# Two mixer layers: level products from 64-row halves, an early copy of one projection, softmax statistics in pairs

## The chip, the cores and the metric

One Trainium2 chip, one NeuronCore. The number is device time in microseconds of one execution of the whole program. TensorE (PE) does the matrix products, VectorE (DVE) and ScalarE (ACT) the element-wise work and everything that leaves PSUM, GpSimd (POOL) some element-wise work between SBUF tiles, SyncE (SP) issues the loads.

## The reference

A float32 model block for 256 tokens and a width of 1024: two layers of a first kind (indexed attention beside a gated delta rule), then two layers of a second kind. The second kind is what is changed. Each of its two layers does

```python
u = rms_norm(h) @ w_in                      # split into the inputs of four mixers
o_a = nsa_attention(...)                    # 4 heads of 64: compressed + selected + window
o_b = diff_attention(...)                   # 4 heads, two softmax maps each, p0 - lam * p1
o_c = gla_mixer(...)                        # 4 heads, key width 32   } chunked gated
o_d = hgrn2_mixer(...)                      # 4 heads, key width 64   } linear attention
h = h + concat(o_a, o_b, o_c, o_d) @ w_out
```

and then a feed-forward part: dense in the first of the two layers, eight experts (two per token) in the second. The two gated linear attentions are, per head, `o_t = sum over s <= t of (q_t . k_s * exp(b_t - b_s)) v_s` within chunks of 64 and a carried state between chunks, with `b` the running sum of the log gates. The differential attention normalises its queries and keys (16 groups of 32 per token) before its products.

## The kernel before, in words

All weight products (`proj_tok`, `proj_ch`, `mm3` at lines 150 to 154) are done as three passes over a high and a low half of the operands; ACT casts the high half (L142) and DVE, or POOL for every fourth one in the mixer layers (`gp_every`), subtracts the low half (L145). The program is written in order with priorities; a planner then fixes the order of the instructions on each engine, and each engine runs its own list strictly in that order. So an instruction that waits holds back all that stands behind it on its engine.

`block2_mixers` (L1186) is run twice. In it:

- **Differential projection** (`ev_dqk`, L1216): for each of the two token tiles the 512 columns in PSUM are squared by ACT, summed by DVE, raised to -1/2 by POOL (`powm`), and then multiplied by DVE straight from PSUM (L1224). The PSUM tile is one of three (`pmm`) that all projections share.
- **Maps** (`softmax_map`, L1410; `nsa_a`, `diff_a`): eight items per layer, four of each kind, each with two logit tiles. Each logit tile gets its own maximum (DVE, L1413), scaling (DVE, L1414) and two exponentials with a running sum (ACT, L1418); then come reciprocals and scalings per tile, transposes (PE, L1426) and the product with the values (PE, L1459, L1495). An item's first half is put ahead of the second half of the item before it (`staggered`). The maps have a priority ahead of the levels.
- **Levels** (L1616): the causal matrix within blocks of 128 tokens is built in seven levels with half-widths s = 1, 2, 4, ..., 64, and one product for the two blocks against each other (`Ex`, L1663 on). At each level, decays `E` are formed by two subtractions (DVE, L1624 and L1626) and one exponential over both halves (ACT, L1631); the decayed keys `Kt` are written by POOL (L1634); the decayed queries `Q` by DVE (L1636); `queries` (L1605) spreads them by six ACT copies (L1610 four, L1613 two) into zero-filled tiles `qbg`, `qbh`, in which each head has a column block of its own with only its rows filled. The products (L1647 for `gla`, L1649 for `hgrn2`) then contract over all 128 rows. Their results go from the two `gd` buffers of PSUM into `AT`: by four predicated copies of DVE (L1659) for s up to 16, by ACT copies (L1655) for 32 and 64. So one level's results must leave before the next level's products may start. `AT` itself is first filled with the diagonal: `pgk`, a product on POOL (L1588), small matrix products into `dg`, and two POOL instructions of 128x1024 (L1599).
- The output `gpo` (L1716) takes `AT`, and the result goes through `w_out` (`tile_T`, `proj_tok`).
- Weight loads of later stages wait for their buffers, which come free as the projections are split.

Of the kernel before, what the change touches and what calls it, by code (L numbers as in the profile page):

```python
# [10 lines left out]
F32 = mybir.dt.float32  # L11
# [1114 lines left out]
def level_tiles(k):  # L1126

    k.qbg = k.lvl.tile([P, 2, 4, P], F32, tag="qbg", name="qbg")
    k.qbh = k.lvl.tile([P, 2, 2, 2, P], F32, tag="qbh", name="qbh")
    k.AT = k.lvl.tile([P, 2, 8, P], F32, tag="AT", name="AT")  # L1130
    k.nc.gpsimd.memset(k.qbg, 0.0)
    k.nc.gpsimd.memset(k.qbh, 0.0)


def prepare_b2(k):
# [25 lines left out]
    for l, r in enumerate(k.r2):  # L1161
        lam_init = 0.8 - 0.6 * math.exp(-0.3 * l)
        nc.vector.tensor_scalar(r.on[:, 0, :], r.on[:, 0, :], 1.0 - lam_init, None, op0=ALU.mult)
        lv = r.lam.rearrange("p (a b d) -> p a b d", a=2, b=2)
        pr = cp.tile([P, 2, 32], F32, name=f"lamp{l}")
        nc.vector.tensor_tensor(pr, lv[:, :, 0, :], lv[:, :, 1, :], op=ALU.mult)
        s2 = cp.tile([P, 2], F32, name=f"lams{l}")
        nc.vector.tensor_reduce(s2, pr, axis=AX.X, op=ALU.add)
        nc.scalar.activation(s2, s2, AF.Exp)
        r.nlam = cp.tile([P, 1], F32, name=f"nlam{l}")  # L1170
        nc.vector.tensor_sub(r.nlam, s2[:, 1:2], s2[:, 0:1])
        nc.vector.tensor_scalar(r.nlam, r.nlam, lam_init, None, op0=ALU.subtract)

# [12 lines left out]
def block2_mixers(k, a, l, hl, pre):  # L1186
# [5 lines left out]
    with ExitStack() as es:  # L1192
# [23 lines left out]
        def ev_dqk(tt, ps):  # L1216
            sq = n2("dsq").rearrange("p (g d) -> p g d", d=32)
            nc.scalar.activation(sq, ps.rearrange("p (g d) -> p g d", d=32), AF.Square)
# [4 lines left out]
            dqk = n2("dqk").rearrange("p (g d) -> p g d", d=32)  # L1223
            nc.vector.tensor_tensor(dqk, ps.rearrange("p (g d) -> p g d", d=32),  # L1224
                                    r[:, :, None].to_broadcast([P, 16, 32]), op=ALU.mult)
# [184 lines left out]
        def softmax_map(lp, S, n, sc, name):  # L1410

            mx = sm.tile([P, n], F32, tag="mx", name="mx", bufs=8)
            nc.vector.tensor_reduce(mx, lp, axis=AX.X, op=ALU.max)  # L1413
            nc.vector.tensor_scalar(mx, mx, -sc, None, op0=ALU.mult)  # L1414
            su = sm.tile([P, n], F32, tag="su", name="su", bufs=12)
            pr = n2(name).rearrange("p (n s) -> p n s", n=n)
            for j in range(n):
                nc.scalar.activation(pr[:, j, :S], lp[:, j, :], AF.Exp, scale=sc, bias=mx[:, j : j + 1],  # L1418
                                     accum_out=su[:, j : j + 1])
            return pr, su  # L1420
# [11 lines left out]
        def nsa_a(kind, tt, m):  # L1432
# [9 lines left out]
            r = []  # L1442
            for j in range(2):
                pr, su = softmax_map(lps[j][:, :, :S], S, 2, 0.125, "npr")
                nc.vector.reciprocal(su, su)
                nc.vector.tensor_tensor(su, su, g3[:, tt, 2 * m + j, 1:3], op=ALU.mult)
                r.append((pr, su))
            return r
# [18 lines left out]
        def diff_a(kind, tt, par):  # L1467
# [10 lines left out]
            e0, s0 = softmax_map(lps[0][:, :, :S], S, 2, dsc, "de0")  # L1478
            e1, s1 = softmax_map(lps[1][:, :, :S], S, 2, dsc, "de1")
            nc.vector.reciprocal(s1, s1)  # L1480
            nc.vector.scalar_tensor_tensor(s1, s1, r2.nlam, s0, op0=ALU.mult, op1=ALU.mult)
            nc.vector.reciprocal(s0, s0)
# [5 lines left out]
        def diff_b(r, kind, tt, par):  # L1488
# [12 lines left out]
            if par == 1:  # L1501
# [8 lines left out]
                for g in range(4):  # L1510
                    o = mv[:, g]
                    nc.vector.scalar_tensor_tensor(o, o, ss[:, g : g + 1], r2.on[:, 0, :], op0=ALU.mult, op1=ALU.mult)
# [9 lines left out]
        gcat = one.tile([P, 3, T], F32, name="gcat")  # L1522
        gf = lambda t: t.rearrange("p a t -> p (a t)")
# [64 lines left out]
        nc.gpsimd.tensor_tensor(pgk, qcat, kcat, op=ALU.mult)  # L1588
        dgp = gdt("dg")[:, :16].rearrange("p (t h) -> p t h", t=2)
        for tt in range(2):  # L1590
            sl = slice(tt * P, (tt + 1) * P)
            nc.tensor.matmul(dgp[:, tt, 0:4], pgk[:, 0, sl], c["bd32"], start=True, stop=True)
            for cb in range(2):
                nc.tensor.matmul(dgp[:, tt, 4 + 2 * cb : 6 + 2 * cb], pgk[:, 1 + cb, sl], c["bd64"],
                                 start=True, stop=True)
        dg = one.tile([P, 2, 8], F32, name="dg")
# [6 lines left out]
        AX_ = one.tile([P, 8, P], F32, name="ATx")  # L1603

        def queries(i, src):  # L1605

            Qg, Qh = k.qbg[:, i % 2], k.qbh[:, i % 2]
            for h in range(4):
                rows = slice(32 * h, 32 * h + 32)
                nc.scalar.copy(Qg[rows, h, :], src[rows, 0, :])  # L1610
# [3 lines left out]
            return Qg, Qh  # L1614

        for i, s in enumerate(LEVELS):  # L1616
# [3 lines left out]
            bv, Ev = pv(b_), pv(E)  # L1620
            if s == 64:
                nc.scalar.activation(Ev[:, :, 1, :], bv[:, :, 1, :], AF.Exp)
            else:
                nc.vector.tensor_tensor(Ev[:, :, 1, :], bv[:, :, 1, :],  # L1624
                                        bv[:, :, 0, s - 1 : s].to_broadcast([P, npair, s]), op=ALU.subtract)
            nc.vector.tensor_tensor(Ev[:, :, 0, :], bv[:, :, 0, s - 1 : s].to_broadcast([P, npair, s]),  # L1626
                                    bv[:, :, 0, :], op=ALU.subtract)
            if s == 64:
                nc.scalar.activation(Ev[:, :, 0, :], Ev[:, :, 0, :], AF.Exp)
            else:  # L1630
                nc.scalar.activation(E, E, AF.Exp)  # L1631

            Kt = Kts[i % 2]
            nc.gpsimd.tensor_tensor(pv(Kt)[:, :, 0, :], pv(kcat)[:, :, 0, :], Ev[:, :, 0, :], op=ALU.mult)  # L1634
            Q = sm.tile([P, 3, P], F32, tag="Q", name="Q")
            nc.vector.tensor_tensor(gf(Q).rearrange("p (n s) -> p n s", s=s), pv(qcat)[:, :, 1, :], Ev[:, :, 1, :],  # L1636
                                    op=ALU.mult)
            Qg, Qh = queries(i, Q)
            od4 = lambda ap: ap.rearrange("p h (b two s) -> p h b two s", two=2, s=s)[:, :, :, 1, :]
            bs = lambda ap: ap.rearrange("p (b s) -> p b s", s=s)  # L1640
            bs4 = lambda ap: ap.rearrange("p h (b s) -> p h b s", s=s)
            pg = gdt("pg").rearrange("p (t h i) -> p t h i", t=2, h=4)
            ph = gdt("ph").rearrange("p (t h i) -> p t h i", t=2, h=4)
            for tt in range(2):
                sl = slice(tt * P, (tt + 1) * P)
                hs = slice(tt * 64, (tt + 1) * 64)
                nc.tensor.matmul(pg[:, tt], Kt[:, 0, sl], Qg[:, :, hs], start=True, stop=True)  # L1647
                for cb in range(2):
                    nc.tensor.matmul(ph[:, tt, 2 * cb : 2 * cb + 2], Kt[:, 1 + cb, sl], Qh[:, cb, :, hs],  # L1649
                                     start=True, stop=True)  # L1650
            for o, ps in ((0, pg), (4, ph)):
                if s >= 32:

                    for b in range(0, P, 2 * s):
                        nc.scalar.copy(k.AT[b : b + s, :, o : o + 4, b + s : b + 2 * s],  # L1655
                                       ps[b : b + s, :, :, b // 2 : b // 2 + s])
                    continue
                for tt in range(2):
                    nc.vector.copy_predicated(od4(k.AT[:, tt, o : o + 4, :]),  # L1659
                                              bs(k.lvm[s])[:, None].to_broadcast([P, 4, 64 // s, s]),  # L1660
                                              bs4(ps[:, tt]))
# [12 lines left out]
        nc.gpsimd.tensor_tensor(Kt[:, :, :P], kcat[:, :, :P], E[:, :, :P], op=ALU.mult)  # L1674
        Q = sm.tile([P, 3, P], F32, tag="Q", name="Qx")
        nc.vector.tensor_tensor(Q, qcat[:, :, P:], E[:, :, P:], op=ALU.mult)
        Qg, Qh = queries(len(LEVELS), Q)
        pg = gdt("pgx").rearrange("p (h i) -> p h i", h=4)
        ph = gdt("phx").rearrange("p (h i) -> p h i", h=4)
        nc.tensor.matmul(pg, Kt[:, 0, :P], Qg, start=True, stop=True)  # L1680
        for cb in range(2):
            nc.tensor.matmul(ph[:, 2 * cb : 2 * cb + 2], Kt[:, 1 + cb, :P], Qh[:, cb], start=True, stop=True)
# [475 lines left out]
```

## Time and profile before

| | us |
|---|---|
| three runs, median (lowest to highest) | 2425.89 (2424.93 to 2430.03) |
| profiled execution, whole | 2425.61 |
| its span, first to last instruction | 2423.5 |
| first mixer layer, in the span | about 693 to 890 |
| second mixer layer, in the span | about 1163 to 1345 |
| mean granted TensorE clock | 0.986 of full speed |

A busy share is the time in which an engine had an instruction under way. A busy PE is not a PE at its peak, and it counts time at the lower clock in full. Idle time of an engine is named after what ended it. Times in the rows below are microseconds from the start of the span unless a column says ns. Line numbers are those of the kernel before.

### The profile page before, as it was taken

What the parts mean: (1) busy time and instruction counts of PE and PEld (TensorE: products, weight loads), DVE (VectorE), ACT (ScalarE), POOL (GpSimd) and SP (SyncE); (2) the same over time, 40 slices, a digit from 0 to 9 for tenths busy, and PEclk for the clock granted to TensorE, in tenths of its full rate; (3) what the DMA queues carried; (4) which work ended last, traced back from release to release, by engine and by line L of the source; (5) the groups of instructions that cost most, each with busy time, mean ns of one, the idle gap of its engine ahead of it and who ended that gap; (6) DMA issues with size and microseconds to landing.
All of it is one profiled execution on the core that took longest, in us unless ns stands there. A gap on an engine that the chain in (4) does not pass through costs nothing. (4 is left out here: it accounts for less than half of the span.)

```text
span 2423.5 us, 35194 instructions
## 1 busy us (share of the span) xinstructions
PE 2324.4 (96%) x13123; PEld 1949.1 (80%) x13123; DVE 1873.6 (77%) x2844; ACT 1491.0 (62%) x2333; POOL 408.9 (17%) x424
## 2 busy tenths in 40 slices
PE   8999999999999799999988999999999999999997
PEld 7898879888878689998776787887878777877775
DVE  5958576776766855556577799989998989898985
ACT  5455454455545754445466677777777777776763
POOL 3534114532142321111432100000000000000000
PEclk9999999999999899999999999999999999999998
DMA  8343254343346135555540999999999999999972
GB/s 249 105 139 123 88 170 158 122 140 108 128 153 199 40 131 180 186 189 182 164 157 25 351 364 345 371 331 364 361 349 330 354 345 346 346 350 348 345 256 88
DMA packets 288735, 550.07 MB, mean 227 GB/s; under 512 B 17414, under 2 KB 95020, under 8 KB 288300
## 3 DMA queue, kind: packets, MB, share of 16 engines
q1 hardware_dynamic: 287372, 546.67, 64.4%
q8 instruction: 105, 1.72, 0.3%
q0 software_dynamic: 144, 1.05, 0.1%
q14 instruction: 74, 0.61, 0.1%
q10 hardware_dynamic: 1040, 0.03, 0.0%
HBM read 545.61 MB, written 2.10 MB: 226 GB/s over the span
## 5 line engine op out<-in xcount | busy, mean ns | idle before, releaser
L145 DVE TENSOR_TENSOR wlo<-raw,whi 128x1024 fp32r<-128x1024 f32 x948 | 1143.2, 1236 | 267.8 <-ACT whi L142 260.5
L142 ACT CAST whi<-raw 128x1024 fp32r<-128x1024 f32 x984 | 1009.0, 1048 | 436.8 <-PE pt L153 92.1
L151 PE MATMUL pt<-whi,xh 128*128 128x512 f32 (+3 forms) x656 | 251.5, 395 | 14.6 <-DVE q L612 3.0
L152 PE MATMUL pt<-wlo,xh 128*128 128x512 f32 (+3 forms) x656 | 257.3, 393 | 2.9 <-DVE wlo L145 2.6
L153 PE MATMUL pt<-whi,xl 128*128 128x512 f32 (+3 forms) x656 | 253.0, 387 | 0.0
L243 POOL TENSOR_TENSOR nr<-nms,pwm 128x1 f32<-128x1 f32 x16 | 8.7, 547 | 1135.1 <-DVE nms L258 1135.0
L152 PE MATMUL mg<-wlo,xg 128*128 128x512 f32 x448 | 180.4, 403 | 3.3 <-DVE wlo L145 3.3
L152 PE MATMUL mu<-wlo,xg 128*128 128x512 f32 x448 | 179.1, 400 | 3.1 <-DVE wlo L145 3.1
L152 PE MATMUL ya<-wlo,hh 128*128 128x512 f32 x448 | 177.5, 397 | 0.1
L151 PE MATMUL mg<-whi,xg 128*128 128x512 f32 x448 | 177.2, 396 | 0.0
L153 PE MATMUL mg<-whi,xg 128*128 128x512 f32 x448 | 177.1, 395 | 0.0
L151 PE MATMUL mu<-whi,xg 128*128 128x512 f32 x448 | 177.0, 395 | 0.0
L153 PE MATMUL mu<-whi,xg 128*128 128x512 f32 x448 | 176.9, 395 | 0.0
L153 PE MATMUL ya<-whi,hl 128*128 128x512 f32 x448 | 175.8, 393 | 0.0
L151 PEld LDWEIGHTS pt<-whi,xh 128*128 128x128 f32 x656 | 124.9, 192 | 40.9 <-issue 8.7
L151 PE MATMUL pc<-xh,whi 128*128 128x256 f32 (+1 forms) x496 | 143.9, 290 | 5.8 <-DVE q L611 2.2
L152 PEld LDWEIGHTS pt<-wlo,xh 128*128 128x128 f32 x656 | 126.0, 192 | 28.4 <-DVE wlo L145 5.5
L151 PE MATMUL ya<-whi,hh 128*128 128x512 f32 x448 | 140.6, 394 | 5.6 <-ACT whi L142 5.6
L153 PEld LDWEIGHTS pt<-whi,xl 128*128 128x128 f32 x656 | 125.2, 191 | 22.8 <-DVE xl L284 1.1
L152 PE MATMUL pc<-xl,whi 128*128 128x256 f32 (+1 forms) x496 | 142.8, 288 | 0.0
L153 PE MATMUL pc<-xh,wlo 128*128 128x256 f32 (+1 forms) x496 | 142.7, 288 | 0.0
L151 PE MATMUL gu<-xh,whi 128*128 128x256 f32 x448 | 126.7, 283 | 0.0
(643 smaller groups left out, 4718.0 us busy)
## 6 DMA issues: line engine op xcount, KB each, us to landing
raw<-in_moe_w_gate SPq DMA_DIRECT2D x112, 1024.0 KB, 6.8
raw<-in_moe_w_up SPq DMA_DIRECT2D x112, 1024.0 KB, 6.7
raw<-in_moe_w_down SPq DMA_DIRECT2D x112, 1024.0 KB, 6.7
raw<-in_w_in SPq DMA_DIRECT2D x92, 1024.0 KB, 5.1
raw<-in_w_out SPq DMA_DIRECT2D x16, 1024.0 KB, 5.0
raw<-in_ffn_w_gate SPq DMA_DIRECT2D x14, 1024.0 KB, 5.1
raw<-in_ffn_w_up SPq DMA_DIRECT2D x14, 1024.0 KB, 5.3
raw<-in_ffn_w_down SPq DMA_DIRECT2D x14, 1024.0 KB, 5.6
```

What stands on the lines that cost most here:

```text
L142: nc.scalar.copy(hi, raw_view)
L145: k.last_split = eng.tensor_sub(lo, raw_view, hi)
L151: nc.tensor.matmul(out, lh, rh, start=start, stop=False)
L152: nc.tensor.matmul(out, lh, rl, start=False, stop=False)
L153: return nc.tensor.matmul(out, ll, rh, start=False, stop=stop)
L243: return k.nc.gpsimd.tensor_tensor(out, in_, k.pw[e][:, :n], op=ALU.pow)
```

## The change

- **Levels.** The zero-filled query tiles and their memsets go. A tile `lq` holds the decayed queries compactly; two DVE multiplications write it: one from `qm`, two copies of the `gla` queries in which ACT has zeroed every other block of 32 rows (scale `gm`), and one from the two `hgrn2` blocks. Each product now contracts over 64 rows; a pair for rows 0 to 63 and 64 to 127 stands one behind the other and goes to two PSUM tiles. Twelve products per level take the place of six, with the same number of columns in all.
- `Kt` is written by DVE instead of POOL, and not at all at s = 1, where `kcat` itself serves. At s = 2 to 32 `E` is one subtraction over both halves and two exponentials over one half each. The predicated copies are two per level, twice as wide.
- **Diagonal.** `pgk` moves from POOL to DVE. `AT` is filled by 16 ACT copies of 128x128 with a scale per row, instead of two POOL instructions.
- **Differential projection.** ACT copies PSUM to SBUF first; square and multiplication read the copy.
- **Maps.** The two logit tiles of an item share one scaling, one reciprocal and, in `nsa_a`, one gate multiplication: three small DVE instructions fewer per `nsa` item, two fewer per `diff` item. The final norm of the differential output is one DVE and one POOL instruction instead of four of DVE.

```diff
 def level_tiles(k):
-    k.qbg = k.lvl.tile([P, 2, 4, P], F32, tag="qbg", name="qbg")
-    k.qbh = k.lvl.tile([P, 2, 2, 2, P], F32, tag="qbh", name="qbh")
-    k.nc.gpsimd.memset(k.qbg, 0.0)
-    k.nc.gpsimd.memset(k.qbh, 0.0)
-    k.AT = k.lvl.tile([P, 2, 8, P], F32, tag="AT", name="AT")
+    k.lq = k.lvl.tile([P, 2, 4, P], F32, tag="qbg", name="lq")
+    k.AT = k.lvl.tile([P, 2, 4, 2, P], F32, tag="AT", name="AT")
...
         def ev_dqk(tt, ps):
+            dqk = n2("dqk").rearrange("p (g d) -> p g d", d=32)
+            nc.scalar.copy(dqk, ps.rearrange("p (g d) -> p g d", d=32))
-            nc.scalar.activation(sq, ps.rearrange("p (g d) -> p g d", d=32), AF.Square)
+            nc.scalar.activation(sq, dqk, AF.Square)
...
-            nc.vector.tensor_tensor(dqk, ps.rearrange("p (g d) -> p g d", d=32),
-                                    r[:, :, None].to_broadcast([P, 16, 32]), op=ALU.mult)
+            nc.vector.tensor_tensor(dqk, dqk, r[:, :, None].to_broadcast([P, 16, 32]), op=ALU.mult)
...
+        def softmax_maps(lps, S, sc, names):
+            mx = sm.tile([P, 2, 2], F32, tag="mx", name="mx", bufs=4)
+            for i, lp in enumerate(lps):
+                nc.vector.tensor_reduce(mx[:, i], lp[:, :, :S], axis=AX.X, op=ALU.max)
             nc.vector.tensor_scalar(mx, mx, -sc, None, op0=ALU.mult)
...
-                for g in range(4):
-                    o = mv[:, g]
-                    nc.vector.scalar_tensor_tensor(o, o, ss[:, g : g + 1], r2.on[:, 0, :], op0=ALU.mult, op1=ALU.mult)
+                nc.vector.tensor_tensor(mv, mv, ss[:, :, None].to_broadcast([P, 4, 64]), op=ALU.mult)
+                nc.gpsimd.tensor_tensor(mv, mv, r2.on[:, 0:1, :].to_broadcast([P, 4, 64]), op=ALU.mult)
...
+            for d in range(2):
+                nc.scalar.activation(qm[:, d, :], ps, AF.Copy, scale=k.gm[:, d : d + 1])
...
-        nc.gpsimd.tensor_tensor(pgk, qcat, kcat, op=ALU.mult)
+        nc.vector.tensor_tensor(pgk, qcat, kcat, op=ALU.mult)
...
-        for tt in range(2):
-            nc.gpsimd.tensor_tensor(k.AT[:, tt], k.ident[:, None].to_broadcast([P, 8, P]),
-                                dg[:, tt, :, None].to_broadcast([P, 8, P]), op=ALU.mult)
+        for j in range(2):
+            for cc in range(4):
+                for tt in range(2):
+                    nc.scalar.activation(k.AT[:, j, cc, tt], k.ident, AF.Copy, scale=dg[:, j, cc, tt : tt + 1])
...
+        def queries(i, pick, E):
+            q = k.lq[:, i % 2]
+            nc.vector.tensor_tensor(pick(q[:, 0:2]), pick(qm), pick(E[:, 0:1]).to_broadcast(pick(qm).shape), op=ALU.mult)
+            nc.vector.tensor_tensor(pick(q[:, 2:4]), pick(qcat[:, 1:3]), pick(E[:, 1:3]), op=ALU.mult)
+            return q
+        def products(ps, Kt, q, sl, hs, out):
             for j in range(2):
                 rows = slice(64 * j, 64 * j + 64)
-                nc.scalar.copy(Qh[rows, :, j, :], src[rows, 1:3, :])
+                nc.tensor.matmul(out(ps[j][:, 0:2]), Kt[rows, 0, sl], q[rows, 0:2, hs], start=True, stop=True)
+            for cb in range(2):
+                for j in range(2):
+                    rows = slice(64 * j, 64 * j + 64)
+                    nc.tensor.matmul(out(ps[j][:, 2 + cb]), Kt[rows, 1 + cb, sl], q[rows, 2 + cb, hs],
+                                     start=True, stop=True)
...
+                nc.vector.tensor_tensor(p2(E), p2(b_), p2(b_)[:, :, s - 1 : s].to_broadcast([P, npair, 2 * s]),
+                                        op=ALU.subtract)
+                nc.scalar.activation(Ev[:, :, 1, :], Ev[:, :, 1, :], AF.Exp)
+            if s > 1:
+                nc.scalar.activation(Ev[:, :, 0, :], Ev[:, :, 0, :], AF.Exp, scale=-1.0)
...
+            q = queries(i, pick, E)
+            if s > 1:
+                nc.vector.tensor_tensor(pv(Kt)[:, :, 0, :], pv(kcat)[:, :, 0, :], Ev[:, :, 0, :], op=ALU.mult)
+            ps = [gdt(f"pg{j}").rearrange("p (c t i) -> p c t i", c=4, t=2) for j in range(2)]
```

## Rows read from the trace of the kernel before

**Rows 1.** The page, its first part: busy time, share and instructions by engine.
```profile
PE 2324.4 (96%) x13123; PEld 1949.1 (80%) x13123; DVE 1873.6 (77%) x2844; ACT 1491.0 (62%) x2333; POOL 408.9 (17%) x424
```

**Rows 2.** Stretches: length, busy PE, PEld, DVE, ACT, POOL (instructions), clock, DMA share, GB/s.
```profile
712.00:719.20 7.20, 5.43 (x13) 4.30 (x14) 2.72 (x4) 1.04 (x1) 5.19 (x4) 0.53 0.00 0
...
786.00:826.00 40.00, 31.23 (x148) 24.49 (x147) 38.98 (x73) 28.46 (x66) 18.12 (x15) 0.82 0.18 60
826.00:850.00 24.00, 20.52 (x104) 15.62 (x103) 11.87 (x39) 17.08 (x50) 3.72 (x4) 0.81 0.00 1
...
900.00:1100.00 200.00, 200.00 (x1411) 187.38 (x1410) 104.24 (x119) 87.51 (x118) 32.70 (x24) 1.00 0.54 185
...
1256.00:1300.00 44.00, 34.37 (x173) 25.95 (x171) 42.46 (x85) 33.33 (x86) 20.39 (x15) 0.92 0.16 54
```

**Rows 3.** PE's waits in the mixer layers: us in total, times, longest.
```profile
PE pg L1647 <- ACT qbg L1610: 4.1, 1, 4.1
PE pg L1647 <- DVE AT L1659: 2.9, 1, 2.9
PE pt L151 <- DVE dqk L1224: 2.2, 1, 2.2
...
PE pg L1647 <- DVE AT L1659: 5.2, 2, 4.5
PE pt L151 <- DVE dqk L1224: 0.8, 2, 0.4
```

**Rows 4.** Timeline of DVE and POOL, first layer: start, us, engine, line, operation, tiles.
```profile
790.01 0.56 DVE L1626 TENSOR_TENSOR E<-gcat 128x384 f32<-128x384 f32 x1
794.07 2.25 DVE L1626 TENSOR_TENSOR E<-gcat 128x384 f32<-128x384 f32 x1
802.33 2.71 DVE L1636 TENSOR_TENSOR Q<-qcat,E 128x384 f32<-128x384 f32 x1
830.15 0.76 DVE L1659 COPY_PREDICATED AT<-lvm,pg 128x256 f32<-128x256 uint32 x2
...
793.76 4.31 POOL L1599 TENSOR_TENSOR AT<-cst,dg 128x1024 f32<-128x1024 f32 x2 [0.18 <-DVE dg L1597]
801.95 2.67 POOL L145 TENSOR_TENSOR wlo<-raw,whi 128x1024 fp32r<-128x1024 f32 x1
```

**Rows 5.** Groups of instructions from 786 to 862: busy, mean ns, idle before them.
```profile
L1610 ACT COPY qbg<-Q 32x128 f32<-32x128 f32 x28 | 8.3, 295 | 7.2 <-PE pg L1647 3.7 <-DVE Q L1636 3.0
L1634 POOL TENSOR_TENSOR Kt<-kcat,E 128x384 f32<-128x384 f32 x7 | 8.1, 1158 | 13.1 <-ACT E L1629 6.1 <-PE ph L1649 3.9 <-ACT E L1631 3.1
L1636 DVE TENSOR_TENSOR Q<-qcat,E 128x384 f32<-128x384 f32 x7 | 7.7, 1102 | 0.0
L1626 DVE TENSOR_TENSOR E<-gcat 128x384 f32<-128x384 f32 x7 | 6.5, 930 | 0.0
L1613 ACT COPY qbh<-Q 64x256 f32<-64x256 f32 x14 | 5.6, 403 | 3.5 <-PE ph L1649 3.2
L1624 DVE TENSOR_TENSOR E<-gcat 128x384 f32<-128x384 f32 x6 | 4.0, 667 | 0.0
```

**Rows 6.** Timeline of ACT: one exponential with a per-row operand.
```profile
779.75 0.37 ACT L1418 ACTIVATE npr<-nl,mx 128x128 f32<-128x128 f32 x1 [2.82 <-DVE mx L1414]
```

**Rows 7.** Timeline of PE: a level's products, the tail's steps, a 64-row pair.
```profile
810.56 1.02 PE L1647 MATMUL pg<-qbg,Kt 128*128 128x256 f32 x4
...
812.23 0.48 PE L153 MATMUL pt<-whi,xl 128*128 128x512 f32 x1
...
828.09 2.02 PE L1647 MATMUL pg<-qbg,Kt 128*128 128x256 f32 x4
...
848.23 1.02 PE L1680 MATMUL pgx<-qbg,Kt 128*128 128x512 f32 x2
...
850.88 0.70 PE L1439 MATMUL nl<-nkTs,nqT 64*128 64x256 f32 x4
851.52 0.28 PE L1441 MATMUL nl<-ntrib,identb 128*128 128x128 bf16 x2
```

More of the change, by code (lines that the diff above doesn't have):

```diff
@@ L1172, in prepare_b2 @@
         nc.vector.tensor_scalar(r.nlam, r.nlam, lam_init, None, op0=ALU.subtract)
+    k.gm = cp.tile([P, 2], F32, name="gm")
+    nc.vector.tensor_tensor(k.gm, k.c["bd32"][:, 0:2], k.c["bd32"][:, 2:4], op=ALU.add)
+    nc.vector.tensor_scalar(k.gm, k.gm, 32**-0.5, None, op0=ALU.mult)
     k.lvm = {}
@@ L1441, in nsa_a @@
                     nc.tensor.matmul(lps[j][:, n, S - P : S], k.identb, k.ntrib, start=False, stop=True)
[L1442 to L1448, printed above, removed]
+            prs, su = softmax_maps(lps, S, 0.125, ("npr", "npr"))
+            nc.vector.reciprocal(su, su)
+            nc.vector.tensor_tensor(su, su, g3[:, tt, 2 * m : 2 * m + 2, 1:3], op=ALU.mult)
+            return [(prs[j], su[:, j]) for j in range(2)]
         def nsa_b(r, kind, tt, m):
@@ L1477, in diff_a @@
                     nc.tensor.matmul(lps[cc][:, n, S - P : S], k.identb, k.ntrib, start=False, stop=True)
[L1478 to L1482, printed above, removed]
+            (e0, e1), su = softmax_maps(lps, S, dsc, ("de0", "de1"))
+            s1 = sm.tile([P, 2], F32, tag="ds1", name="ds1", bufs=4)
+            rs = sm.tile([P, 2, 2], F32, tag="drs", name="drs", bufs=4)
+            nc.vector.reciprocal(rs, su)
+            nc.vector.scalar_tensor_tensor(s1, rs[:, 1], r2.nlam, su[:, 0], op0=ALU.mult, op1=ALU.mult)
+            s0 = rs[:, 0]
             for n in range(2):
@@ L1522, in block2_mixers @@
         gcat = one.tile([P, 3, T], F32, name="gcat")
+        qm = one.tile([P, 2, T], F32, name="qm")
         gf = lambda t: t.rearrange("p a t -> p (a t)")
@@ L1593, in block2_mixers @@
             for cb in range(2):
-                nc.tensor.matmul(dgp[:, tt, 4 + 2 * cb : 6 + 2 * cb], pgk[:, 1 + cb, sl], c["bd64"],
-                                 start=True, stop=True)
-        dg = one.tile([P, 2, 8], F32, name="dg")
+                nc.tensor.matmul(dgp[:, :, 2 + cb, tt], pgk[:, 1 + cb, sl], c["bd64"], start=True, stop=True)
+        dg = one.tile([P, 2, 4, 2], F32, name="dg")
         nc.vector.tensor_copy(dg, dgp)
-        for tt in range(2):
-            nc.gpsimd.tensor_tensor(k.AT[:, tt], k.ident[:, None].to_broadcast([P, 8, P]),
-                                dg[:, tt, :, None].to_broadcast([P, 8, P]), op=ALU.mult)
@@ L1603, in block2_mixers @@
[L1603 to L1610, printed above, removed]
+        for j in range(2):
+            for cc in range(4):
+                for tt in range(2):
+                    nc.scalar.activation(k.AT[:, j, cc, tt], k.ident, AF.Copy, scale=dg[:, j, cc, tt : tt + 1])
+        AX_ = one.tile([P, 2, 4, P], F32, name="ATx")
@@ L1620, in block2_mixers @@
             bv, Ev = pv(b_), pv(E)
+            Kt = kcat if s == 1 else Kts[i % 2]
             if s == 64:
                 nc.scalar.activation(Ev[:, :, 1, :], bv[:, :, 1, :], AF.Exp)
-            else:
[L1624 to L1643, printed above, removed]
-            for tt in range(2):
[L1645 to L1650, printed above, removed]
@@ new lines, in block2_mixers, with pick @@
+            if s > 1:
+                nc.scalar.activation(Ev[:, :, 0, :], Ev[:, :, 0, :], AF.Exp, scale=-1.0)
+            def pick(t):
+                if t.shape[2] == P:
+                    return t.rearrange("p a (n s) -> p a n s", s=s)
+                return t.rearrange("p a (n two s) -> p a n two s", two=2, s=s)[:, :, :, 1, :]
+            q = queries(i, pick, E)
+            if s > 1:
+                nc.vector.tensor_tensor(pv(Kt)[:, :, 0, :], pv(kcat)[:, :, 0, :], Ev[:, :, 0, :], op=ALU.mult)
@@ L1652, in block2_mixers @@
+            ps = [gdt(f"pg{j}").rearrange("p (c t i) -> p c t i", c=4, t=2) for j in range(2)]
+            for tt in range(2):
+                products(ps, Kt, q, slice(tt * P, (tt + 1) * P), slice(tt * 64, (tt + 1) * 64),
+                         lambda o: o[:, :, tt] if len(o.shape) == 4 else o[:, tt])
+            for j in range(2):
                 if s >= 32:
                     for b in range(0, P, 2 * s):
-                        nc.scalar.copy(k.AT[b : b + s, :, o : o + 4, b + s : b + 2 * s],
-                                       ps[b : b + s, :, :, b // 2 : b // 2 + s])
+                        nc.scalar.copy(k.AT[b : b + s, j, :, :, b + s : b + 2 * s],
+                                       ps[j][b : b + s, :, :, b // 2 : b // 2 + s])
@@ L1657, in block2_mixers @@
                     continue
[L1658 to L1661, printed above, removed]
+                nc.vector.copy_predicated(
+                    k.AT[:, j].rearrange("p c t (b two s) -> p (c t) b two s", two=2, s=s)[:, :, :, 1, :],
+                    k.lvm[s].rearrange("p (b s) -> p b s", s=s)[:, None].to_broadcast([P, 8, 64 // s, s]),
+                    ps[j].rearrange("p c t (b s) -> p (c t) b s", s=s))
@@ L1673, in block2_mixers @@
         Kt = Kts[len(LEVELS) % 2]
[L1674 to L1682, printed above, removed]
-        nc.scalar.copy(AX_[:, 0:4, :], pg)
-        nc.scalar.copy(AX_[:, 4:8, :], ph)
+        nc.vector.tensor_tensor(Kt[:, :, :P], kcat[:, :, :P], E[:, :, :P], op=ALU.mult)
+        q = queries(len(LEVELS), lambda t: t if t.shape[2] == P else t[:, :, P:], E)
+        ps = [gdt(f"px{j}").rearrange("p (c i) -> p c i", c=4) for j in range(2)]
+        products(ps, Kt, q, slice(0, P), slice(0, P), lambda o: o)
+        for j in range(2):
+            nc.scalar.copy(AX_[:, j], ps[j])
         last, tc.cur_priority = tc.cur_priority, first
```

36 lines of the change are left out of this document (20 added, 16 removed).

## The prediction

> **What bounds the kernel now.** I read the page first, then the busy times by stretch, then PE's waits inside the weak stretches, then the timelines of the engines named there. PE is under way 96% of the span [rows 1], so outside the two mixer layers the kernel is PE's own work: in the dense feed-forward stretch PE is busy 200.00 of 200 us at full clock, and DVE about half of that [rows 2]. Whatever the mixers save therefore moves all that follows forward; nothing there takes it back, as the later loads wait for buffers that come free with the same work.
>
> Two kinds of stretch lose PE time [rows 2]. From 786 to 826, the levels' first part, PE is busy 31.23 of 40 us at a clock of 0.82, while DVE is busy 38.98: DVE sets the pace, and ACT at 28.46 does not. From 1256 to 1300 it is the same in the second layer (PE 34.37, DVE 42.46 of 44). From 826 to 850 nobody is full: PE 20.52 of 24 at 0.81, DVE 11.87, ACT 17.08. That is the levels' tail, a chain. The waits say the same: PE's longest are for ACT's query copies (4.1) and for DVE's predicated copies (2.9, and 5.2 in the second layer) [rows 3]. [...]
>
> The profiled execution took 2425.61 us, of which 2423.5 are span; the median of the runs is 0.28 above it. I sum against 2425.6 and give the median's forecast 0.3 higher.
>
> **DVE in the saturated part.** A 384-wide subtraction takes 0.56 us when POOL is quiet and 2.25 when POOL is filling `AT` (4.31 us) [rows 4]. POOL's instructions with SBUF inputs stretch DVE's. How much: in the three groups of E and Q, seven at 1.102, seven at 0.930 and six at 0.667 [rows 5], against 0.55 each, the excess is 3.9 + 2.7 + 0.7 = 7.3 us. One instruction of 2.71 in it belongs to a weight split on POOL (2.67) [rows 4], which stays: 2.2 off, 5.1 left. That is the lower end for what the removed POOL work costs DVE. The upper end is all of that POOL time, 4.3 for `AT` and 8.1 for `Kt` [rows 4, 5], 12.4. I take 7, nearer the lower end, since much of `Kt` runs where DVE has slack (the tail).
>
> [...]
>
> DVE takes on: `Kt` at two or three of the levels that fall in this part (0.56 each [rows 4], 1.5); the queries in two instructions of 256 instead of one of 384, at the same rate 0.75 instead of 0.56, four times (0.8). It gives up one of two subtractions at s = 1 (0.56) and some small instructions and the split norm (together between 0 and 1.5, taken as 0.7). `pgk` lies before this part. Net +1.0. So DVE's load falls by about 6 us per layer, and with DVE full this shortens the stretch by as much: **12 us** for both layers. ACT does not take over: it loses, per level, four copies of 295 ns and two of 403 [rows 5], 2.0 us, so 8 over four levels, and gains 16 scaled copies of 0.30 to 0.37 (a 32-row copy [rows 5] and an exponential with a per-row operand [rows 6]), 4.8 to 5.9, beside two `qm` copies and a split exponential, together under 2.
>
> **The tail.** From the product at s = 8 to the cross product 20.1 us pass for four steps (828.09 to 848.23) [rows 7], 5.0 a step. What a step can't go under is what holds the two PSUM buffers: the products, 1.67 us (810.56 to 812.23 [rows 7]), and the predicated copies, two pairs of 0.76 [rows 4], 3.2 in all. The six ACT copies leave the chain, where they stood between DVE's product and PE, and `Kt` leaves POOL. Both halves of a level now end together, so the copying of one no longer lies beside the products of the other; this keeps me from the floor. I take the middle, 4.1: 0.9 a step, 3.6 a layer, **7 us** for both, with ends at 0 and 14.
>
> **The products.** The trace shows no run of different 64-row pairs behind each other, so both ends. Two 64-row products of 256 columns take 0.64 us side by side (850.88 to 851.52), where two 128-row ones take half of a level's 1.67, 0.84 [rows 7]. So the pair does run side by side; the rest of the 0.64 over its columns' time, some 0.2, may fall on every pair or only where the row form changes. On every pair, a token tile's three pairs (128, 64 and 64 columns) take 0.42, 0.31 and 0.31, a level 2.1; on the first alone, a level takes 1.1. Over 16 levels that is +6.6 or -9; I take **0**, as PE does not set the pace there. The cross product is counted as a level.
>
> **Differential projection.** PSUM comes free after one ACT copy instead of after the chain over POOL. ACT is idle there (1.04 of 7.2 us [rows 2]), so the copy costs nothing; if ACT were full it would cost its own length before each square. The wait of 2.2 goes. The 5.43 us of PE at 0.53 would be 2.7 shorter at full clock. Together 4.9 at most; next late is the weight stream, so I take 4, and 0.8 for the second layer [rows 3]: **4.8**.
>
> **Maps and norm.** Some 20 small DVE instructions fewer per layer are counted above. The first two exponentials of an item now wait for the second tile's maximum; queued behind them on ACT are weight casts, for which PE waits. As both tiles' products end together, I cost it at nothing; its cover is that ACT is not full. The norm's second step on POOL lies before the last transposes of the layer: about a quarter of the 2.15 us of a 1024-wide instruction [rows 4], 0.5 a layer, **+1**. Two memsets less and `gm` cost or save nothing: POOL idles, and DVE is not full before 786.
>
> **Sum.** 2425.6 - 12 - 7 - 4.8 + 0 + 1 = 2402.8; for the median **2403**.
>
> **Rivals.**
>
> 1. *PE gets all of it.* If DVE and ACT both fall below PE's need, the idle time of [rows 2] goes (8.8 + 3.5 in the first layer, 9.6 in the second) and so does the lower clock: at 0.82 over 40 us PE spent 14.4 us at half speed, 7.2 lost, at 0.81 over 24 us 4.6, at 0.92 over 44 us 1.8. With the projection's 5.7 that is 41 us. Four fifths of it give 2393. For it: DVE full and half of the excess of someone else's making. Against it: the order on the engines is planned anew, and no plan hits every wait.
> 2. *The maps set the tail.* The last map's first product starts at 850.88, right behind the cross product [rows 7], and twelve microseconds of map follow. If the maps' own chain (maximum, exponentials, transposes) is the length of the tail, the levels' gain turns into waiting: only half of the 12, and the 4.8, remain: 2415. Against: PE's named waits are for levels, not for maps [rows 3].
> [...]
> 4. *ACT becomes the bound, and it is slower.* The 16 scaled copies (4.8 to 5.9 us a layer) must be done before the first predicated copy, and weight casts of the running projections stand behind them on ACT. If ACT is full around 794, PE loses some 5 us a layer and drops to the lower clock as it did after 712, 2.7 more; `AT` is late, so the levels gain nothing. 2425.6 + 15.4 - 4.8 = 2436. It decides when ACT's busy share around the `dg` copy passes about 95%. For it: these copies are many and small. Against: ACT is at 28.46 of 40 there and loses 8.
> 5. *A part does not do what it says* (DVE's order puts `Kt` and queries behind weight splits, so nothing comes earlier): the projection's 4.8 alone, 2421.
>
> **How the numbers follow.** Chances: forecast 0.50 (2397 to 2410), rival 1 0.15 (2385 to 2397), rival 2 0.13 (2410 to 2420), rival 3 0.07, rival 4 0.09, rival 5 0.06. A measurement of this kernel tells about 0.2%, 4.9 us, from no change. Faster by more than that: all of the forecast and rivals 1 and 3, most of rival 2, a third of rival 5: 0.83. The same: 0.08; slower: 0.09. For eight in ten I take 2388 to 2420: it leaves out rivals 4 and 5 and the far end of rival 1.
>
> **What would show it.** Right: DVE's subtractions at 0.55 us beside no POOL; busy DVE in the first part about 33 us instead of 39; steps of the tail near 4 us; no wait for `dqk` and no clock below 0.9 behind it; six ACT copies per level gone. Wrong: PE waiting for whi casts behind the 16 copies; steps of 5 us with the waits now named after maps; level products over 1.9 us at full clock; a new order in which a level's products stand behind a map that waits.

## The result and the profile after

| kernel | median of its runs, us | range | profiled execution, its span |
|---|---|---|---|
| before | 2427.43 | 2424.93 to 2430.03 | 2425.61, 2423.5 |
| after | 2455.65 | 2454.58 to 2456.74 | 2455.73, 2453.9 |

The ratio is 1.0116, 95% interval [1.0104, 1.0128]: the change costs 28 us where the forecast had it save 23. Differences below are between medians, against the kernel before on the same chip (2427.4 to 2429.3 us). The first part of the page of after, which answers to [rows 1], and the stretches of [rows 2] in after with three more (columns as there):

```profile
PE 2371.3 (97%) x13303; PEld 1997.9 (81%) x13303; DVE 1867.7 (76%) x2794; ACT 1471.6 (60%) x2287; POOL 378.9 (15%) x402
```
```profile
712.00:719.20 7.20, 7.20 (x35) 6.03 (x34) 4.90 (x7) 2.65 (x4) 7.20 (x4) 1.00 0.37 113
786.00:826.00 40.00, 34.94 (x193) 27.59 (x193) 34.72 (x65) 20.13 (x57) 8.99 (x7) 0.76 0.16 56
826.00:850.00 24.00, 24.00 (x121) 19.70 (x119) 9.82 (x28) 10.12 (x29) 0.00 (x0) 0.50 0.00 1
900.00:1100.00 200.00, 199.54 (x1403) 187.74 (x1404) 106.78 (x123) 90.48 (x125) 31.63 (x23) 1.00 0.55 185
...
807.00:871.70 64.70, 64.00 (x298) 55.03 (x299) 33.24 (x80) 20.89 (x59) 8.96 (x9) 0.50 0.00 1
872.00:892.00 20.00, 17.51 (x86) 13.98 (x85) 10.79 (x19) 10.69 (x19) 5.14 (x3) 1.00 0.49 158
1281.40:1352.90 71.50, 70.34 (x332) 59.02 (x332) 39.55 (x95) 25.04 (x67) 8.47 (x9) 0.50 0.01 5
```

Much of the forecast is there. The projection's stretch, 0.53 before, is at full clock with PE busy throughout. DVE fell from 38.98 to 34.72 of 40 us in the first part, ACT from 28.46 to 20.13, and PE idles 5 us there where it idled 9. But from 807 to 871.7 and from 1281.4 to 1352.9 the granted clock is 0.50, with PE busy 64.00 of 64.70 and 70.34 of 71.50 us. At full clock these 134.3 busy microseconds would be some 67, an estimate that halves all of them by that 0.50. DVE and ACT, relieved, idle beside it (33.24 and 20.89 busy of 64.70). PE, which had 3.5 us of idle time from 826 to 850 before [rows 2], now has none: it is the bound of both tails. PE's waits for the levels in the first tail, and its timeline, say how that began and ended:

```profile
PE pg L1622 <- DVE AT L1668: 3.2, 1, 3.2
PE pg L1622 <- DVE Kt L1656: 1.5, 1, 1.5
```
```profile
789.98 0.49 PE L1622 MATMUL pg<-lq,kcat 64*128 64x128 f32 x4
790.30 0.56 PE L1626 MATMUL pg<-lq,kcat 64*128 64x64 f32 x8
790.70 0.44 PE L1622 MATMUL pg<-lq,kcat 64*128 64x128 f32 x4
790.97 0.56 PE L1626 MATMUL pg<-lq,kcat 64*128 64x64 f32 x8
791.46 0.50 PE L152 MATMUL pt<-wlo,xh 128*128 128x512 f32 x1
...
807.70 0.79 PE L1622 MATMUL pg<-lq,Kt 64*128 64x128 f32 x2 [3.24 <-DVE AT L1668]
...
813.79 0.79 PE L1622 MATMUL pg<-lq,Kt 64*128 64x128 f32 x2
...
846.46 1.22 PE L1622 MATMUL px<-lq,Kt 64*128 64x256 f32 x2
...
854.21 1.92 PE L1721 MATMUL gpo<-vv,AT 128*128 128x64 f32 x8
...
868.47 0.78 PE L151 MATMUL pt<-whi,xh 128*128 128x512 f32 x1
...
871.96 0.48 PE L151 MATMUL pt<-whi,xh 128*128 128x512 f32 x1
```

A level's products take 1.48 us at full clock (789.98 to 791.46), a little under before's 1.67 [rows 7]. After a short wait for `Kt` PE waits 3.24 us for the predicated copies and has the lower clock when it resumes. Before had the like (2.9 and 5.2 [rows 3]) and got its clock back: in its first tail 0.50 from 820 to 830, 1.00 from 845 to 855. After gets it back only where the output projection's 128x512 products have begun (868.47; 1.00 from 872 on). The last level product (`px`, from 846.46) is over at 849.6, so some 20 us of the stretch hold map products and `gpo`, most of them 128-row products of 64 columns; the clock does not come back under them either (0.50 from 849.6 to 868.4). The four steps of the tail, from s = 8 (813.79) to `px`, take 32.7 us, 8.2 a step, where the forecast had 4.1.

### The profile page after: what moved, and what is told of

It is laid out like the page before. It is cut to its first block, busy times and chain, and to the rows that moved or that the text cites. A ratio compares the mean times of both kernels' runs of the same rounds, so it can differ in the third digit from the quotient of the medians.

```text
span 2453.9 us, 35379 instructions
## 1 busy us (share of the span) xinstructions
PE 2371.3 (97%) x13303; PEld 1997.9 (81%) x13303; DVE 1867.7 (76%) x2794; ACT 1471.6 (60%) x2287; POOL 378.9 (15%) x402
## 5 line engine op out<-in xcount | busy, mean ns | idle before, releaser
L153 PE MATMUL gu<-xh,wlo 128*128 128x256 f32 x448 | 127.0, 283 | 0.0
```

Of the source, the lines that this page charges most:

```text
L153: return nc.tensor.matmul(out, ll, rh, start=False, stop=stop)
```

## The experiments

**Theory A**: the 64-row products themselves hold the clock at the lower level. **Theory B**: the new order and its waits do it, whatever the form of the products. For each kernel, the time, its ratio to the kernel before on the same chip, and the mean granted clock over 780 to 900 and 1240 to 1400, which hold the two tails:

| kernel | us | ratio, interval | clock, clock |
|---|---|---|---|
| before | 2427.43 | | 0.90, 0.97 |
| after | 2455.65 | 1.0116 [1.0104, 1.0128] | 0.73, 0.78 |
| rows128 | 2422.86 | 0.9973 [0.9963, 0.9983] | 0.87, 0.93 |
| rows128_maps | 2419.01 | 0.9957 [0.9942, 0.9972] | 0.91, 0.94 |
| before_rows64 | 2464.25 | 1.0148 [1.0132, 1.0163] | 0.73, 0.78 |
| levels_alone | 2473.22 | 1.0177 [1.0160, 1.0194] | 0.69, 0.74 |
| dense_fill | 2491.52 | 1.0242 [1.0219, 1.0266] | 0.69, 0.71 |
| burst | 2444.23 | 1.0069 [1.0054, 1.0085] | 0.79, 0.83 |
| full_rows | 2416.74 | 0.9949 [0.9935, 0.9963] | 0.89, 0.90 |
| full_wide | 2416.76 | 0.9955 [0.9942, 0.9969] | 0.93, 0.93 |
| others_alone | 2430.14 | 0.9998 [0.9985, 1.0011] | 0.91, 0.90 |
| dqk_alone | 2422.62 | 0.9970 [0.9959, 0.9982] | 0.96, 0.94 |
| pairs_alone | 2436.04 | 1.0033 [1.0021, 1.0046] | 0.93, 0.91 |
| pairs_only | 2436.61 | 1.0034 [1.0022, 1.0046] | 0.93, 0.93 |
| norm_alone | 2426.31 | 0.9992 [0.9983, 1.0001] | 0.93, 0.94 |
| wide_alone | 2414.46 | 0.9951 [0.9937, 0.9965] | 0.96, 0.98 |
| wide_dqk | 2403.49 | 0.9900 [0.9885, 0.9915] | 0.97, 0.96 |

An edit of one thing in the program is not one thing on the engines: the planner orders each kernel's instructions anew. burst nearly keeps the order of after, and dqk_alone that of before; in most other pairs the lists differ in the tails (in rows128 PE runs 36 level records from 808.39 on before it turns to a map, in after 24 from 807.70 on). So a single pair does not rule out that the new order has a share in its difference; four pairs for the 64-row products that agree, on different surroundings (after and rows128, after and full_rows, before and before_rows64, wide_alone and levels_alone), make it unlikely that this share is large.

**The rows of the products.** In `products` of after:

```
-nc.tensor.matmul(out(ps[j][:, 0:2]), Kt[rows, 0, sl], q[rows, 0:2, hs], ...)
+nc.tensor.matmul(out(ps[j][:, 0:2]), Kt[:, 0, sl], q[:, 0:2, hs], ...)
(the hgrn products likewise)
```

> The kernel after, with one thing changed: each product of a level (and of the cross block) takes all 128 rows of the weights and of the queries, not 64; count, columns, order and waits stay. The sums run over both halves, so the mixers' values differ. Theory A (the 64-row products keep TensorE's clock at the lower level once a wait has dropped it): the granted clock comes back within some 15 us, as in the kernel before; the two stretches of 65 and 72 us at 0.50 shrink below 30 us each, and the time falls to 2410 to 2430 us, though two products no longer run side by side. Theory B (the order and the waits of the new chain drop the clock, whatever the products' rows): both stretches stay above 55 us, and the time is 2455 to 2475 us.

Measured: 2422.86, 33 us under after. A wait of 3.08 us for `AT` still stands ahead of the fall in the first tail, but the lower clock now lasts 27 us there and 17 + 7 us in the second:

```profile
808.70:836.00 27.30, 27.30 (x118) 24.23 (x117) 17.34 (x42) 6.35 (x19) 5.84 (x4) 0.50 0.00 1
1276.40:1293.50 17.10, 14.12 (x68) 13.71 (x68) 15.87 (x39) 5.18 (x15) 3.29 (x4) 0.50 0.06 15
1303.70:1310.50 6.80, 6.80 (x34) 6.12 (x33) 3.15 (x10) 2.52 (x9) 0.00 (x0) 0.50 0.00 0
```

Theory B's numbers did not come, and A's time and stretches did, except that the clock took 27 and 17 us to come back, not 15. In the first stretch PE is busy for all of 27.30 us, mostly with 128-row products: the row count is not the whole of it.

The converse edits the kernel before alone: the same 64 rows per head pair, in twice as many products of half the columns, into two banks. The heads' places in `AT` follow, and DVE's list comes out in another order; the rest of the program is kept.

```
+for j, ps in enumerate((pg, ph)):
+    r = slice(64 * j, 64 * j + 64)
+    nc.tensor.matmul(ps[:, tt, 0:2], Kt[r, 0, sl], Qg[r, 2 * j : 2 * j + 2, hs], ...)
(hgrn likewise)
```

> The kernel before with one thing changed: each head pair's product as 64 rows of the same zero-filled queries, two banks, 6 products per token block for 3; the chain on VectorE, ScalarE and POOL, the maps and the projection stay. Theory A: this alone brings the loss: a stretch of 50 us or more at the lower clock in each tail and 2450 to 2475 us. Theory B (the new chain's order and waits bring it): low stretches as in the kernel before, and 2425 to 2440 us.

Measured: 2464.25, 36 us more than before, by this edit of the program alone; the tails' clocks are those of after. Two stretches of its first tail and one of its second (columns as in [rows 2]):

```profile
826.00:850.00 24.00, 22.55 (x127) 19.07 (x124) 13.78 (x42) 15.55 (x47) 4.71 (x5) 0.60 0.00 1
850.00:872.00 22.00, 22.00 (x102) 18.79 (x102) 5.22 (x20) 7.41 (x19) 1.62 (x2) 0.50 0.00 1
...
1300.00:1340.00 40.00, 39.89 (x203) 32.01 (x202) 24.23 (x66) 22.05 (x62) 7.34 (x7) 0.57 0.02 7
```

The levels' part by itself (the hunks of the change outside projection, maps and norm):

> The kernel before with only the levels' part of the change (64-row products, compact queries, Kt and pgk on VectorE, the diagonal on ScalarE); projection, maps and norm as before. Theory A: all of the loss is here, 2450 to 2465 us, with the lower clock for over 55 us in each layer's tail. Theory B with the waits made by the maps' pairs: the wait for AT stays below 2 us, the clock comes back, 2415 to 2430 us.

Measured: 2473.22, 43.9 us more than before and beyond A's range; after lost 28.2. All of the loss is in this part. That the other parts took some 16 us off it in after, while they gain nothing by themselves (below), is explained only in part: levels_alone still has the projection's wait (2.1 us), and by the clocks in the table its two stretches lose some 11 us more than after's. Why their clock is lower is open.

**What drops the clock, and what raises it.** Two kernels add products that are overwritten later, ahead of the real ones in the same bank:

```
+def dense(out, n):
+    for _ in range(n):
+        nc.tensor.matmul(out.rearrange(...), k.identb, k.identb[:, None, :].to_broadcast([P, 4, P]), ...)
dense_fill:  +for t in raw: dense(t, 2)      (each level)   +dense(t, 1)  (each map)
burst:       +if s == 16: dense(raw[0], 12)
```

> The kernel after with work added that is overwritten: two 128x512 bf16 products into each of a level's two banks and one into each of a map's two banks ahead of the real ones (44 per layer, 88 in all; at 0.22 us each some 19 us of TensorE at full clock). Theory A: these full-array products bring the clock back, the low stretches shrink below 35 us each, and the time falls in spite of the added work, to 2425 to 2445 us. Theory B, or a TensorE that is bound by its own count of work: the clock stays low in the tails and the time grows by the added work, 2465 to 2495 us.

> The kernel after with twelve 128x512 bf16 products back to back (overwritten later) in one place of each layer, ahead of the fifth level's products: some 5 us at the lower clock. Theory A1 (full-array work without a break raises the clock, and the 64-row work after it drops it again with no wait needed): the clock rises during or right after the burst in both layers, falls again within 20 us, and low time per tail is 45 to 70 us; 2450 to 2465 us. Theory A2 (only a wait drops it): it rises at the burst and stays up, low time per tail 25 to 40 us, 2430 to 2445 us. Theory A3 (such bf16 products don't count, whatever their row): no rise, 2462 to 2475 us.

dense_fill missed A's numbers: 2491.52 and the clock still low. The time lies in the other range, which B shares with a TensorE bound by its own work, so this run does not decide between A and B. Spread among 64-row products, such work did not raise the clock for 68 us, and its time adds up. It does say something of the fall: 10 us at full clock with PE idle 0.56 us in all, and then the fall:

```profile
810.70:820.70 10.00, 9.44 (x64) 6.78 (x63) 10.00 (x22) 4.30 (x9) 4.06 (x3) 1.00 0.10 26
820.90:889.00 68.10, 67.53 (x270) 52.58 (x269) 21.81 (x60) 15.97 (x44) 5.15 (x4) 0.50 0.00 1
```

burst puts the same products in one place, and both directions show. PE's timeline around the burst, then the stretches before, between and behind:

```profile
820.30 0.95 PE L1634 MATMUL pg<-lq,Kt 64*128 64x64 f32 x4
821.19 4.88 PE L1196 MATMUL pg<-identb 128*128 128x512 bf16 x12
826.00 0.49 PE L1630 MATMUL pg<-lq,Kt 64*128 64x128 f32 x2
...
834.49 0.70 PE L1485 MATMUL dl<-dT 32*128 32x256 f32 x4
835.12 0.28 PE L1487 MATMUL dl<-ntrib,identb 128*128 128x128 bf16 x2
835.34 0.86 PE L1485 MATMUL dl<-dT 32*128 32x256 f32 x4
836.13 0.39 PE L1487 MATMUL dl<-ntrib,identb 128*128 128x128 bf16 x2
836.46 0.79 PE L1630 MATMUL pg<-lq,Kt 64*128 64x128 f32 x2
```
```profile
805.10:825.40 20.30, 19.59 (x74) 14.54 (x75) 15.62 (x35) 5.83 (x17) 4.00 (x4) 0.50 0.00 1
825.60:835.70 10.10, 10.10 (x82) 8.05 (x79) 6.11 (x16) 5.18 (x15) 0.00 (x0) 1.00 0.01 2
835.90:866.40 30.50, 30.50 (x147) 26.97 (x146) 9.78 (x26) 9.84 (x27) 3.99 (x4) 0.50 0.00 1
```

The clock rises at the end of twelve full-array products in a row, stays up for 10 us, and falls with PE busy 10.10 of 10.10 us: here no wait was needed. That is A1, and so is the time at the lower clock, 51 and 55 us in the two tails. The second layer shows the rise too, behind nine of the products in a row (from 1293.35), but two waits (0.71 and 1.44 us) stand before its fall. Only the time was better than A1 gave, 2444.23, inside A2's range: the twelve products cost about 5 us a layer and took 11 us net off the kernel.

**Products of full rows with right values.** The queries are laid into zero-filled tiles by two ScalarE copies a level:

```
+nc.scalar.copy(k.lz[j][rows, i % 2], q[rows])
-nc.tensor.matmul(out(ps[j][:, 0:2]), Kt[rows, 0, sl], q[rows, 0:2, hs], ...)
+nc.tensor.matmul(out(ps[j][:, 0:2]), Kt[:, 0, sl], q[j][:, 0:2, hs], ...)
```

> The kernel after, with the heads' queries laid into two zero-filled tiles (two ScalarE copies of 64 rows per level) so that every level product takes all 128 rows and the values stay those of the reference. Theory A: as rows128 but for two copies of some 0.5 us per level on ScalarE, which is idle three quarters of that time: 2420 to 2428 us, low clock below 35 us in each tail. If the copies come on the path: 2428 to 2440 us. If rows128 gained by its values or by work left out: 2450 us or more.

Measured: 2416.74, a little better than expected: the first version with the reference's values that is faster than both kernels. So what rows128 gained does not come from its values. In the second tail, though, the clock stayed low for 31 us with 128-row level products through most of it (PE waits 2.99 us for `AT` near its start):

```profile
1268.80:1299.30 30.50, 27.51 (x129) 25.74 (x129) 25.56 (x54) 14.65 (x33) 5.33 (x5) 0.50 0.03 10
```

So rows are not all of it, as in rows128. These products are still narrow, 128 and 64 columns for each load of weights. full_wide gives back before's width (the heads' places and the copies into the zero-filled tile follow):

```
+nc.tensor.matmul(out(ps[0]), Kt[:, 0, sl], q[:, 0:4, hs], ...)
+nc.tensor.matmul(out(ps[1][:, cb::2]), Kt[:, 1 + cb, sl], q[:, 4 + cb :: 2, hs], ...)     (cb = 0, 1)
```

> full_rows with the products wide again as in the kernel before: one 128-row product of 256 columns for the four gated heads and two of 128 columns for the others, per token block (3 in place of 6). A level then has 12 matmul records where full_rows and the kernel after have 24; before's level took 2.04 us of TensorE at full clock, theirs takes 2.68 us. Theory A with the width in it (rows and columns per weight load both count): the low clock per tail falls below 20 us and the time to 2403 to 2412 us. Theory A by rows alone: only the 0.6 us per level go, where TensorE sets the pace (some 20 to 25 us at the lower clock): 2412 to 2417 us. If the order of the copies or the strided outputs cost: 2418 us or more.

Measured: 2416.76, the upper end of "rows alone". (Two of the expectation's durations were misread: at full clock a level takes 1.67 us in before and 1.48 in after; only full_rows needs some 2.7.) The width raised the clock (0.84 and 0.85 to 0.90 and 0.88) and took 15 us off PE's busy time over both stretches, but PE's idle time in them grew by as much. Stretches 786 to 872 and 1256 to 1356, full_rows and then full_wide:

```profile
786.00:872.00 86.00, 80.35 (x475) 68.55 (x474) 58.33 (x127) 52.25 (x128) 15.11 (x12) 0.84 0.13 42
1256.00:1356.00 100.00, 90.09 (x529) 78.57 (x527) 62.70 (x136) 60.16 (x144) 17.47 (x14) 0.85 0.29 104
```
```profile
786.00:872.00 86.00, 71.03 (x390) 57.06 (x390) 60.96 (x127) 53.56 (x131) 16.93 (x12) 0.90 0.16 52
1256.00:1356.00 100.00, 84.42 (x469) 67.94 (x468) 67.10 (x154) 61.76 (x146) 21.67 (x15) 0.88 0.33 119
```

rows128_maps asks whether the maps' own 64- and 32-row products hold the clock down as well (`qT[rows, m, sl]` to `qT[:, m, sl]`, `dT[rows, ...]` to `dT[:, ...]`):

> rows128, and also the maps' score products (64 rows and 32 rows) taken with all 128 rows; same count and columns, the values differ. Theory A, for any product of few rows: the low clock left in the tails (27 and 24 us in rows128) shrinks below 15 us each and the time falls to 2405 to 2418 us. If only the wait for AT ahead of it makes that low clock: no change, 2419 to 2426 us.

Measured: 2419.01, the lower end of "no change". It is 4 us under rows128, but the intervals of the two ratios overlap, so no gain is shown. The clock, too, was low for longer than A's 15 us, with no product of few rows left in the levels or the maps:

```profile
807.10:824.20 17.10, 16.75 (x75) 16.02 (x76) 14.07 (x34) 4.24 (x14) 5.84 (x4) 0.50 0.00 1
1271.30:1291.80 20.50, 17.15 (x76) 16.52 (x77) 15.83 (x38) 5.17 (x15) 2.63 (x3) 0.50 0.04 12
```

**The other parts.** Each is the change's own hunks on the kernel before:

> The kernel before with only the other parts of the change (early copy of the differential projection, maxima and sums in pairs, norm's gain on POOL); the levels as before. Theory A: some 5 us faster than before by the projection's wait that is gone, 2418 to 2426 us, low clock in the tails as before (under 25 us per layer). Theory that these parts cost part of the loss: 2432 us or more.

> The kernel before with the early copy of the differential projection alone. The forecast's part d: the wait of 2.16 us and the lower clock behind it go, 4.8 us less, 2422 to 2425 us. If the time is given back at the next wait of the chain: 2427 to 2431 us, with TensorE's wait for dqk gone and the levels' waits longer by as much.

> The kernel before with the maps' maxima and sums in pairs and norm's gain on POOL alone. The forecast's parts b and e: 6 us less, 2420 to 2425 us. If the tail isn't set by VectorE's steps: 2427 to 2432 us. A pair that waits for two maps' exponentials and makes the chain later: 2433 us or more.

others_alone came out at 2430.14, between its two ranges and no gain; its halves cancel: dqk_alone 6.1 us less, pairs_alone 7.3 us more. Splitting the latter:

> The kernel before with only norm's gain moved to POOL (two instructions in place of four, one of them on POOL). The forecast's part e: 1 us more, 2428 to 2432 us. If this is what makes pairs_alone 7.3 us slower (POOL's wait stands ahead of Kt's multiplication in its queue): 2433 us or more.

> The kernel before with only the maps' maxima and sums in pairs, norm as before. The forecast's part b: 7 us less, 2419 to 2424 us. If the pairs are what costs (the first map's exponentials wait for the second one's maximum): 2432 to 2438 us. If norm does: 2426 to 2431 us.

The pairs cost 8.3 us; norm's move measured 2.0 us less, not to be told from nothing. ACT's waits from 1256 to 1356, pairs_only, suggest where the pairs bite (us in total, times, longest); in the same stretch of before, ACT waited for `mx` once, 3.4 us:

```profile
ACT npr L1421 <- DVE mx L1415: 5.3, 1, 5.3
ACT de L1421 <- DVE mx L1415: 3.6, 1, 3.6
```

The first exponential of an item now waits for the maximum of the second bank as well, on a DVE that is full (42.09 of 44 us from 1256). In the first tail (786 to 872) PE waits 7.2 us for `dptT`, which comes behind those exponentials, 1.1 before:

```profile
PE dpo L1497 <- ACT dptT L1432: 7.2, 2, 5.1
```

The engines' order is another one here as well, and the sums and reciprocals are in pairs too. That the shared maximum is what costs is the likely reading and was not tested by itself.

**The parts that gain, together.** wide_alone is the kernel before with full_wide's levels; wide_dqk adds the early copy of the projection to it, with maps and norm as before.

> The kernel before with the chain of the levels from the change (multiplications, pgk and diagonal taken off POOL, compact queries) but with before's wide 128-row products from zero-filled tiles; projection, maps and norm as before. If the relief of VectorE from POOL is what is left of the forecast's gain (its part a, 12 us): 2412 to 2420 us. If it is hidden like the rest: 2424 to 2432 us.

> The kernel before with the two parts that gained by themselves: the levels' chain with wide 128-row products (wide_alone, 14.3 us under the kernel before) and the early copy of the differential projection (dqk_alone, 6.1 us under it); maps and norm as before. If the parts add: 2406 to 2411 us, the fastest of all. If they remove the same waiting: 2412 to 2417 us.

wide_alone: 14.3 us less (11.9 by the ratio). wide_dqk: 2403.49, 24.9 us less and the fastest of all. That is 2.5 us below the range for parts that add; with the intervals it can't be told from the two parts' 20.4. The two stretches in it:

```profile
786.00:872.00 86.00, 75.61 (x428) 60.80 (x427) 62.96 (x147) 56.51 (x134) 20.14 (x14) 0.96 0.22 77
1256.00:1356.00 100.00, 87.77 (x493) 70.60 (x492) 73.15 (x179) 61.43 (x129) 15.08 (x12) 0.93 0.46 164
```

## Why the prediction was wrong, step by step

- **DVE in the saturated part, 12 us, and the tail, 7 us: right in direction, too large together.** wide_alone holds both and gained 14.3 us where they promised 19. In its tail the four steps from s = 8 to the cross product take 15.4 and 17.8 us in the two layers, 3.9 and 4.5 a step where I had 4.1; before's take 20.1 [rows 7] and 19.1:

  ```profile
  1291.69 1.10 PE L1647 MATMUL pg<-qbg,Kt 128*128 128x256 f32 x4
  1310.80 1.02 PE L1680 MATMUL pgx<-qbg,Kt 128*128 128x512 f32 x2
  ...
  822.01 2.05 PE L1624 MATMUL pg<-lz,Kt 128*128 128x256 f32 x4 [0.86 <-DVE AT L1667]
  837.45 1.13 PE L1624 MATMUL px<-lz,Kt 128*128 128x512 f32 x2 [0.52 <-ACT AT L1664]
  ...
  1283.00 1.10 PE L1624 MATMUL pg<-lz,Kt 128*128 128x256 f32 x4
  1300.83 1.02 PE L1624 MATMUL px<-lz,Kt 128*128 128x512 f32 x2
  ```

  (Before in the second layer, then wide_alone in the first and in the second.) That is 6.0 us, and leaves some 8 of the 12. The clock was higher as well (0.96 and 0.98 in the table above, before 0.90 and 0.97), so how much of either is DVE's relief from POOL is not shown.
- **The products, 0: the step that failed.** "I take 0, as PE does not set the pace there." Their duration at full clock was in the bounds (1.1 to 2.1 us a level; 1.48). What failed is the reason. PE did not set the pace before, where its clock came back between the waits (1.00 from 805 to 815 and again from 845); with 64-row products it did not come back in the tail, and PE set the pace there. I had the low stretches in front of me (0.82 and 0.81 [rows 2]) and booked them as a result of waits, to be won back when the waits go (rival 1). before_rows64 gives the term on the kernel before, +36.0 us; between full_wide and after it is 40, between wide_alone and levels_alone 58. None of the rivals held it: rival 3 looked for the price of the pairs at full clock, where no run shows one (1.48 us a level against before's 1.67), rival 4 on ACT, which fell to 20.13 of 40.
- **The maps, with the pairs' exponentials at nothing: wrong.** The sentence "I cost it at nothing; its cover is that ACT is not full" failed. The pairs measured +8.3 us. ACT was not full, but DVE was, and the second maximum is DVE's, which is the likely reason (above). Rival 2 was set aside because the waits named in [rows 3] are for levels; in the second layer PE waits for the maps as well, which those rows do not show:

  ```profile
  PE npt L1426 <- DVE mix L1499: 3.9, 1, 3.9
  ```
- **Differential projection, 4.8: right**, 6.1 alone, and no wait for `dqk` in any kernel that has the copy. The 2.7 in it are half of PE's 5.43 us: before's clock was 0.51 from 713.7, where the wait ends, to 719.2.
- **Norm, +1:** measured -2.0, not to be told from nothing.
- **Rival 1's sum** has a slip: 0.92 over 44 us loses 3.5 us by the working of its other two stretches, not 1.8, so the whole is 43 and not 41. The half speed in it is before's 0.50 from 820 to 830.

The measured terms add up to -14.3 + 36.0 + 8.3 - 6.1 - 2.0 = +21.9 us; the change measured +28.2. That this comes near is luck. The levels' two terms give +21.7 and measured +43.9 together (levels_alone); the other three give +0.2 and took some 16 off in after. The two misses nearly cancel, so the terms do not add here. wide_dqk comes to 2403.5, the number forecast, but it has wide products and the old maps and norm, and the sum's 12 and 7 were not met one by one: no proof of the method.

At full clock the 64-row products were the faster form: 1.48 us a level against 1.67 [rows 7], and against 2.70 for the same products with 128 rows (800.11 to 802.81 in full_rows). In the tail they ran at 0.50, with PE busy 64.00 of 64.70 us, and that cost far more than the form saved: +36.0 us in before_rows64.

## What to carry to other kernels

A product form is not free because its engine has slack: ask what the clock does under it, by the granted clock of a stretch that already runs such products, and try that one edit by itself first. Splitting 128-row products into 64-row halves saved a tenth of their time at full clock (1.48 us a level for 1.67) and lost the full clock (0.50 for 65 and 72 us); zero rows that fill the array were the cheaper choice (full_wide 2416.76, after 2455.65). And batching two small steps into one saves instructions but makes the first wait for the second's input; in these maps, with DVE full (42.09 of 44 us), the pairs cost 8.3 us. Last, parts measured one by one need not add: where the order is planned anew and the clock moves, measure the combination.

## What was not expected of the hardware

- The clock stayed at 0.50 for 65 and 72 us with PE busy 98 to 99% of the time (after), and fell from 1.00 with no idle time at all (835.8, burst).
- The clock rose behind twelve and behind nine full-array bf16 products in a row (burst), and stayed at 0.50 for 68 us where one or two at a time stood among 64-row products (dense_fill).
- With no product of fewer than 128 rows left in levels and maps, the clock was still at 0.50 for 17 and 21 us (rows128_maps), and with 128-row level products for 27 us with no idle time (rows128). Which property of the products counts these runs leave open.
